# Top-k search of a sparse-attention layer: ties settled tile by tile, the long bit search in a branch of its own

## The chip, the cores and the metric

The kernel runs on one core of one Trainium2 chip. TensorE (PE) multiplies matrices into PSUM, VectorE (DVE) and ScalarE (ACT) work elementwise, GpSimd (POOL) does the same more slowly, SyncE (SP) issues the DMA transfers. Each engine executes its own instructions strictly in the order in which they were written out, and waits on semaphores for the others. The metric is the device time of one execution in microseconds, the median over several runs.

## The reference

One layer of a streaming encoder, for 1024 prompt frames and 64 sample frames (which see 128 cached frames too): a half-step SwiGLU feed-forward block, one combined input projection, a sparse-attention branch and a convolution branch that are gated and merged, an output projection, a second feed-forward block, and a last norm. What the change touches is the choice of keys in the attention branch:

```python
score = jnp.einsum('bqh,bqhs->bqs', wi.astype(jnp.float32), jax.nn.relu(s))
score = jnp.where(admissible[None], score, -jnp.inf)
_, sel = lax.top_k(score, top)          # top = 256 for the prompt, 48 for the sample
valid = sel < limit[None, :, None]
kg = jax.vmap(lambda kb, ib: kb[ib])(k, sel)
vg = jax.vmap(lambda vb, ib: vb[ib])(v, sel)
```

Each query keeps its `top` best keys by an indexer score, the sum over eight heads of a weight times a ReLU. Where several keys have the same score at the border, `top_k` keeps those that come first. A score is exactly zero where all eight ReLUs are zero, so zeros can be tied. The prompt's rows whose `top` covers all admissible keys (the first 256) need no choice.

## The kernel before, in words

All products are made in three passes of split operands (`mm3`, L134 to L138: high by high, high by low, low by high; the copies and differences that split them are L118/L119 and L152/L153). The layer runs in stages: first feed-forward block, input projection piece by piece, indexer scores, search, attention, merge and output projection, second feed-forward block.

The keys are not gathered. Attention works on all keys of a tile of 128 queries, and the search writes a bias row for each query: 0 for a kept key, a huge negative number for the others. The scores of seven tiles stand in `Y` (L653): six prompt tiles with 384, 512, 640, 768, 896 and 1024 keys and the sample's tile of 64 rows with 192 keys, 832 rows in all. The search, L875 to L998, has these steps:

- Fifteen rounds on the upper 16 bits of the scores (L906 to L916) find, for each row, the upper half `hib` of the border score. ScalarE does this for the widest tile, VectorE for the other six.
- The lower halves of the scores that share this upper half are masked out and the eight largest taken (L930, L932). `thr` is the rank wanted among them. For ranks 1 to 7 the lower half of the border score is picked (`lob`), and the next one (`nxt`); for a rank of 8 or more neither is.
- `threshold()` (L939 to L944) joins the halves into the border score `sth`. A row whose `lob` and `nxt` don't differ is either tied or of a rank of 8 or more. The smallest difference over all rows becomes the one flag `deepi` (L947 to L954), by a transpose in 32 x 32 blocks, a reduction, three small copies and a reduction.
- L955 to L960 write the bias of every tile by one comparison, and count the scores below the border.
- If the flag is set (L961, L962), a branch on VectorE alone finds the lower half of every row anew in sixteen rounds, each of which counts over all seven tiles (L979), and then settles the ties of all tiles in seven passes a tile (L986 to L998): a count, an equality, a running sum, a limit, and three passes that turn the running sum into a bias.

The small tiles of the search stand in one PSUM tile, `srch` (L877), out of the pool `lgi`. The pools of PSUM of this stage are closed at L1026, and attention's pools take the same banks; so do the convolution's SBUF buffers (`cvp_`, `ep`, closed at L1025) go to attention's (`ap_`).

While the search runs, TensorE computes gates, 16 of them in 3 chunks of 24 matmul triples each (`gates`, L1013 to L1021: a weight load with its split on ScalarE and GpSimd, products, an eviction by ScalarE at L1019, a store). `GPRE` of them are written ahead of attention (L1023), the rest are the first steps of a background list that attention draws on between its own steps (L1276). GpSimd and ScalarE run the last part of the convolution in the same stretch: ScalarE scales a shifted row (L679), GpSimd adds it (L680).

The order of instructions on each engine is fixed before the run by a planner that goes by priorities and a timeline of its own. What stands in a branch is planned as one unit: nothing from outside is put between its instructions. The search has a raised priority (L875).

## Time and profile before

| what | value |
|---|---|
| median of three runs | 2552.09 us (2544.73 to 2552.24) |
| the profiled execution's own time | 2549.7 us |
| its span | 2547.9 us |
| TensorE busy | 2316.0 us (91%) |
| VectorE busy | 1847.4 us (73%) |
| ScalarE busy | 1164.8 us (46%) |
| GpSimd busy | 1435.6 us (56%) |
| the sixteen rounds' comparisons (L979, 112 of them) | 96.9 us of VectorE |

The span is the time from the first to the last instruction in the trace; the profiled execution took 1.8 us more, and 2.4 us less than the median. The page cuts the span into 40 slices and gives each engine's busy share in tenths. A row of a view of groups names line, engine, operation, output and inputs with their shapes, then the count, the sum of the busy time and the mean of one in nanoseconds. A row of the view of waits says which engine at which line waited for which other engine's line, the total, the number of times and the longest. In a timeline, the first two numbers are the start and the length in microseconds, and a bracket at the end gives the idle time before the instruction and what ended it.

### The profile page before, as it was taken

What the parts mean: (1) busy time and instruction counts of PE and PEld (TensorE: products, weight loads), DVE (VectorE), ACT (ScalarE), POOL (GpSimd) and SP (SyncE); (2) the same over time, 40 slices, a digit from 0 to 9 for tenths busy, and PEclk for the clock granted to TensorE, in tenths of its full rate; (3) what the DMA queues carried; (4) which work ended last, traced back from release to release, by engine and by line L of the source; (5) the groups of instructions that cost most, each with busy time, mean ns of one, the idle gap of its engine ahead of it and who ended that gap; (6) DMA issues with size and microseconds to landing.
All of it is one profiled execution on the core that took longest, in us unless ns stands there. A gap on an engine that the chain in (4) does not pass through costs nothing.

```text
span 2547.9 us, 44592 instructions
## 1 busy us (share of the span) xinstructions
PE 2316.0 (91%) x16762; PEld 2283.4 (90%) x16762; DVE 1847.4 (73%) x4138; ACT 1164.8 (46%) x2237; POOL 1435.6 (56%) x873
## 2 busy tenths in 40 slices
PE   7999999999999999993048989989999999999998
PEld 6999999999999999993048888979999999999998
DVE  7766678766673776899996788557776668767676
ACT  6433345443355568862014555444444345344343
POOL 5455566555466868796045345546555565555554
PEclk9999999999999999997569999989999999999999
DMA  5222323223234432331002245564222222323223
GB/s 181 109 96 96 108 100 118 84 92 108 91 114 137 138 118 87 124 125 46 0 23 68 85 154 164 185 218 144 100 100 92 84 100 84 105 105 118 90 93 110
DMA packets 130408, 273.46 MB, mean 107 GB/s; under 512 B 17936, under 2 KB 77200, under 8 KB 130192
## 3 DMA queue, kind: packets, MB, share of 16 engines
q1 hardware_dynamic: 130192, 270.61, 31.3%
q8 instruction: 132, 2.16, 0.3%
q14 instruction: 84, 0.69, 0.1%
HBM read 231.87 MB, written 38.75 MB: 106 GB/s over the span
## 4 chain that ended last, share of the span: by engine, by line
PE 71%; DVE 16%; DMA 4%; POOL 4%; issue 3%; ACT 2%; SPq 0%; DVEq 0%; ACTq 0%; POOLq 0%
PE ps L136 22%; PE ps L138 22%; PE ps L137 22%; DVE bias L979 4%; POOL ac L680 3%; DMA raw<-wf 1%; PE pt L1093 1%; DMA ga<-d_g 1%; DVE bias L901 1%; DVE ps L312 1%; DVE ga L1230 1%; PE ps L166 1%; DVE x L153 1%; DVE s L314 1%; DVE t L211 1%
## 5 line engine op out<-in xcount | busy, mean ns | idle before, releaser
L119 POOL TENSOR_TENSOR wlo<-raw,whi 128x1024 fp32r<-128x1024 f32 (+1 forms) x187 | 437.3, 2343 | 377.8 <-ACT whi L118 373.9
L136 PE MATMUL ps<-x,whi 128*128 128x272 f32 (+2 forms) x1544 | 484.5, 314 | 137.5 <-DVE sth L944 119.8
L136 PE MATMUL ps<-x,wp 128*128 128x272 f32 x1760 | 506.5, 289 | 3.2 <-ACT wp L152 3.2
L138 PE MATMUL ps<-x,wp 128*128 128x272 f32 x1760 | 503.6, 290 | 2.0 <-DVE wp L153 1.0
L137 PE MATMUL ps<-x,wp 128*128 128x272 f32 x1760 | 505.1, 288 | 0.0
L138 PE MATMUL ps<-x,wlo 128*128 128x272 f32 (+2 forms) x1544 | 481.9, 313 | 0.0
L136 PEld LDWEIGHTS ps<-x,whi 128*128 128x128 f32 x1544 | 294.4, 191 | 140.8 <-DVE sth L944 120.5
L137 PE MATMUL ps<-x,whi 128*128 128x272 f32 (+2 forms) x1334 | 413.7, 310 | 0.9 <-POOL x L153 0.9
L136 PE MATMUL ps<-gh,whi 128*128 128x272 f32 x1408 | 400.1, 289 | 5.6 <-DVE spare L284 3.5
L137 PE MATMUL ps<-gl,whi 128*128 128x272 f32 x1408 | 405.2, 289 | 0.0
L138 PE MATMUL ps<-gh,wlo 128*128 128x272 f32 x1408 | 404.2, 289 | 0.0
L680 POOL TENSOR_TENSOR ac<-ac,pd 128x559 f32<-128x559 f32 x180 | 287.0, 1595 | 157.7 <-ACT pd L679 132.3
L153 POOL TENSOR_TENSOR wlo<-raw,whi 128x1024 fp32r<-128x1024 f32 x88 | 221.4, 2517 | 256.2 <-ACT whi L152 256.2
L136 PEld LDWEIGHTS ps<-x,wp 128*128 128x128 f32 x1760 | 331.2, 188 | 4.2 <-ACT wp L152 4.0
L138 PEld LDWEIGHTS ps<-x,wp 128*128 128x128 f32 x1760 | 328.8, 188 | 3.9 <-DVE wp L153 2.7
L137 PEld LDWEIGHTS ps<-x,wp 128*128 128x128 f32 x1760 | 331.5, 188 | 0.0
L153 POOL TENSOR_TENSOR wp<-s,wp 128x512 fp32r<-128x512 f32 x176 | 256.6, 1458 | 103.3 <-ACT wp L152 103.3
L428 DVE SCALAR_TENSOR_TENSOR h<-ps,h 128x272 f32<-128x272 f32 x384 | 164.4, 438 | 186.9 <-PE ps L138 186.2
L138 PEld LDWEIGHTS ps<-x,wlo 128*128 128x128 f32 x1544 | 294.0, 191 | 1.2
L118 ACT ACTIVATE whi<-raw 128x1024 fp32r<-128x1024 f32 (+1 forms) x187 | 190.5, 1020 | 221.3 <-PE ps L137 110.3
L136 PEld LDWEIGHTS ps<-gh,whi 128*128 128x128 f32 x1408 | 263.5, 189 | 6.9 <-DVE spare L284 3.9
L138 PEld LDWEIGHTS ps<-gh,wlo 128*128 128x128 f32 x1408 | 266.3, 189 | 0.0
(264 smaller groups left out, 5035.6 us busy)
## 6 DMA issues: line engine op xcount, KB each, us to landing
raw<-wf SPq DMA_DIRECT2D x337, 512.0 KB, 3.3
raw<-wf SPq DMA_DIRECT2D x32, 384.0 KB, 3.0
d_g<-sg SPq DMA_DIRECT2D x32, 181.0 KB, 1.9
d_h<-h SPq DMA_DIRECT2D x2, 2176.0 KB, 10.5
y<-t SPq DMA_DIRECT2D x32, 136.0 KB, 1.9
raw<-d_q SPq DMA_DIRECT2D x32, 128.0 KB, 3.5
raw<-d_qi SPq DMA_DIRECT2D x24, 128.0 KB, 3.1
d_g<-sg SPq DMA_DIRECT2D x16, 182.0 KB, 3.3
```

The source lines that it names most:

```text
L118: nc.scalar.activation(hi[:, :n], raw[:, :n], AF.Copy)
L119: self.weng.tensor_tensor(lo[:, :n], raw[:, :n], hi[:, :n], op=ALU.subtract)
L136: t.matmul(out, wh, xh, start=first, stop=False)
L137: t.matmul(out, wh, xl, start=False, stop=False)
L138: t.matmul(out, wl, xh, start=False, stop=last)
L153: (eng or nc.vector).tensor_tensor(lo, x, hi, op=ALU.subtract)
L166: self.nc.tensor.matmul(ps[:, b * P:(b + 1) * P], x[:, t0:t0 + P], self.ones, start=i == 0, stop=i == len(tiles) - 1)
L211: self.nc.vector.scalar_tensor_tensor(x, h[:, k, t0:t0 + w], self.par[:, q:q + 1], r, op0=ALU.mult, op1=ALU.mult)
L312: nc.vector.tensor_tensor(s[2], a0, b0, op=ALU.subtract)
L428: nc.vector.scalar_tensor_tensor(x, p, 0.5, x, op0=ALU.mult, op1=ALU.add)
L680: nc.gpsimd.tensor_tensor(ac, ac, pd, op=ALU.add)
L979: nc.vector.scalar_tensor_tensor(spare(n), Y[:rows, y0:y0 + L], sgn[:rows, c1], cand[:rows, c1].to_broadcast([rows, L]), op0=ALU.mult, op1 ...
```

## The change

The branch behind the flag is cut into nine branches. Inside the outer one the differences `nxt` are copied, and an eighth column is added that says for each row whether its rank is 8 or more while the eighth largest lower half isn't zero (a "far" row). `flags()`, the old reduction made general for up to 32 columns, turns these into eight integers in `tiei`: is any row of this tile tied, and is any row far. A second branch, entered if there is a far row, holds the sixteen rounds as they were, and then writes the bias by a comparison anew. After it, seven branches, one for each tile and each behind a register load of its own, settle the ties of a tile that is flagged: an equality with its sum, two operations on one column, a running sum into a new buffer `rk`, a comparison with the number of ties wanted, and one pass into the bias. The new buffer takes 4 KB a partition. Besides, `GPRE` goes from 10 to 11: one gate more is written ahead of attention, and one less is in the background list.

```diff
@@ -44,7 +44,7 @@
 PAHEAD = 60
 TORD = (7, 6, 8, 5, 4, 3, 2, 1, 0)
 NLG, NPT = 3, 2
-GPRE = 10
+GPRE = 11
 MS = lambda nc: set()
 FILL = {7: 1, 6: 1, 8: 2, 5: 1, 4: 1, 3: 2, 2: 2, 1: 2, 0: 2}
 THI = 6000
@@ -778,6 +778,8 @@
             for j in range(8):
                 nc.gpsimd.memset(rank[:, :, j:j + 1], float(j + 1) if j < 7 else 99.0)
             deepi = kp.tile([1, 1], I32, name="deepi")
+            tiei = kp.tile([1, NT + 1], I32, name="tiei")
+            rk = kp.tile([P, 1024], F32, name="rk")
 
             def cols(g):
                 return slice(COL[g[0]], COL[g[-1]] + 1)
@@ -878,9 +880,9 @@
             thr, low_ = sb_[:, 0:NT], sb_[:, 16:16 + NT]
             hib, lob = sb_[:, 32:32 + NT], sb_[:, 48:48 + NT]
             top8, prod = (sb_[:, a0:a0 + 8 * NT].rearrange("p (n t) -> p n t", t=8) for a0 in (64, 128))
-            deep = sb_[:, 256:328]
-            mi0 = sb_[:, 336:336 + NT].bitcast(I32)
-            nc.vector.memset(sb_[:, 32:328], 0.0)
+            deep = sb_[:, 256:352]
+            mi0 = sb_[:, 352:352 + NT].bitcast(I32)
+            nc.vector.memset(sb_[:, 32:352], 0.0)
             nc.vector.tensor_copy(thr, thr0)
 
 
@@ -945,13 +947,21 @@
             threshold()
 
             nc.vector.tensor_tensor(nxt, lob, nxt, op=ALU.subtract)
+
+            def flags(src, first, dst):
+
+                w = src.shape[1]
+                f = [deep[:, first + 32 * i:first + 32 * i + 32] for i in range(3)]
+                nc.vector.transpose(f[1], f[0])
+                nc.vector.tensor_reduce(f[2][:, 0:1], f[1], axis=AX.X, op=ALU.min)
+                for q in range(1, 4):
+                    nc.vector.tensor_copy(f[2][0:w, q:q + 1], f[2][32 * q:32 * q + w, 0:1])
+                nc.vector.tensor_reduce(f[0][0:w, 0:1], f[2][0:w, 0:4], axis=AX.X, op=ALU.min)
+                nc.vector.transpose(f[1][0:32, :], f[0][0:32, :])
+                nc.vector.tensor_scalar(dst, f[1][0:1, 0:w], 0.5, None, op0=ALU.is_lt)
+
             nc.vector.tensor_reduce(deep[:, 0:1], nxt, axis=AX.X, op=ALU.min)
-            nc.vector.transpose(deep[:, 32:64], deep[:, 0:32])
-            nc.vector.tensor_reduce(deep[:, 64:65], deep[:, 32:64], axis=AX.X, op=ALU.min)
-            for q in range(1, 4):
-                nc.vector.tensor_copy(deep[0:1, 64 + q:65 + q], deep[32 * q:32 * q + 1, 64:65])
-            nc.vector.tensor_reduce(deep[0:1, 68:69], deep[0:1, 64:68], axis=AX.X, op=ALU.min)
-            nc.vector.tensor_scalar(deepi, deep[0:1, 68:69], 0.5, None, op0=ALU.is_lt)
+            flags(deep[:, 0:1], 0, deepi)
             for n in (5, 4, 6, 3, 2, 1, 0):
                 rows, y0, L = rows_of(n)
                 c1 = slice(COL[n], COL[n] + 1)
@@ -962,40 +972,61 @@
             with tc.If(more > 0):
 
 
-                nc.vector.tensor_scalar(flag, hib, float(1 << 15), None, op0=ALU.is_lt)
-                nc.vector.tensor_scalar(sgn, flag, 2.0, -1.0, op0=ALU.mult, op1=ALU.add)
-                nc.vector.tensor_tensor(thr, ktop, lmk, op=ALU.subtract)
-                nc.vector.tensor_tensor(thr, thr, flag, op=ALU.mult)
-                nc.vector.tensor_tensor(thr, thr, lmk, op=ALU.add)
-                nc.vector.memset(lob, 0.0)
-                nc.vector.tensor_copy(low_, lob)
-                for b in range(15, -1, -1):
-                    nc.vector.tensor_scalar(lob, low_, float(1 << b), None, op0=ALU.add)
+                nc.vector.tensor_copy(deep[:, 0:NT], nxt)
+                nc.vector.tensor_scalar(flag, thr, 7.5, None, op0=ALU.is_ge)
+                nc.vector.tensor_tensor(flag, flag, top8[:, :, 7], op=ALU.mult)
+                nc.vector.tensor_reduce(deep[:, NT:NT + 1], flag, axis=AX.X, op=ALU.max)
+                nc.vector.tensor_scalar(deep[:, NT:NT + 1], deep[:, NT:NT + 1], -1.0, 1.0, op0=ALU.mult, op1=ALU.add)
+                flags(deep[:, 0:NT + 1], 0, tiei)
+                far = nc.vector.value_load(tiei[:, NT:NT + 1], min_val=0, max_val=1)
+                with tc.If(far > 0):
+
+                    nc.vector.memset(tiei, 1)
+                    nc.vector.tensor_scalar(flag, hib, float(1 << 15), None, op0=ALU.is_lt)
+                    nc.vector.tensor_scalar(sgn, flag, 2.0, -1.0, op0=ALU.mult, op1=ALU.add)
+                    nc.vector.tensor_tensor(thr, ktop, lmk, op=ALU.subtract)
+                    nc.vector.tensor_tensor(thr, thr, flag, op=ALU.mult)
+                    nc.vector.tensor_tensor(thr, thr, lmk, op=ALU.add)
+                    nc.vector.memset(lob, 0.0)
+                    nc.vector.tensor_copy(low_, lob)
+                    for b in range(15, -1, -1):
+                        nc.vector.tensor_scalar(lob, low_, float(1 << b), None, op0=ALU.add)
+                        threshold()
+                        nc.vector.tensor_tensor(cand, sth, sgn, op=ALU.mult)
+                        for n in VT + (XT,):
+                            rows, y0, L = rows_of(n)
+                            c1 = slice(COL[n], COL[n] + 1)
+                            nc.vector.scalar_tensor_tensor(spare(n), Y[:rows, y0:y0 + L], sgn[:rows, c1],
+                                                           cand[:rows, c1].to_broadcast([rows, L]),
+                                                           op0=ALU.mult, op1=ALU.is_ge, accum_out=cnt[:rows, c1])
+                        nc.vector.tensor_tensor(flag, cnt, thr, op=ALU.is_ge)
+                        nc.vector.scalar_tensor_tensor(low_, flag, float(1 << b), low_, op0=ALU.mult, op1=ALU.add)
+                    nc.vector.tensor_copy(lob, low_)
                     threshold()
-                    nc.vector.tensor_tensor(cand, sth, sgn, op=ALU.mult)
                     for n in VT + (XT,):
                         rows, y0, L = rows_of(n)
                         c1 = slice(COL[n], COL[n] + 1)
-                        nc.vector.scalar_tensor_tensor(spare(n), Y[:rows, y0:y0 + L], sgn[:rows, c1],
-                                                       cand[:rows, c1].to_broadcast([rows, L]),
-                                                       op0=ALU.mult, op1=ALU.is_ge, accum_out=cnt[:rows, c1])
-                    nc.vector.tensor_tensor(flag, cnt, thr, op=ALU.is_ge)
-                    nc.vector.scalar_tensor_tensor(low_, flag, float(1 << b), low_, op0=ALU.mult, op1=ALU.add)
-                nc.vector.tensor_copy(lob, low_)
-                threshold()
-                for n in VT + (XT,):
+                        nc.vector.scalar_tensor_tensor(spare(n), Y[:rows, y0:y0 + L], sth[:rows, c1],
+                                                       negc[:rows].to_broadcast([rows, L]),
+                                                       op0=ALU.is_lt, op1=ALU.mult, accum_out=cnt[:rows, c1])
+
+                for n in (5, 6, 4, 3, 2, 1, 0):
                     rows, y0, L = rows_of(n)
-                    c1 = slice(COL[n], COL[n] + 1)
-                    y, b = Y[:rows, y0:y0 + L], spare(n)
-                    nc.vector.tensor_scalar(b, y, sth[:rows, c1], 0.0, op0=ALU.is_le, op1=ALU.add,
-                                            accum_out=cnt[:rows, c1])
-                    nc.vector.tensor_scalar(need[:rows, c1], cnt[:rows, c1], float(STILES[n][4] - L), None, op0=ALU.add)
-                    nc.vector.tensor_scalar(y, y, sth[:rows, c1], None, op0=ALU.is_equal)
-                    nc.vector.tensor_tensor_scan(y, y, y, 0.0, op0=ALU.add, op1=ALU.bypass)
-                    nc.vector.tensor_scalar(y, y, need[:rows, c1], -NEG, op0=ALU.min, op1=ALU.mult)
-                    nc.vector.scalar_tensor_tensor(b[:, 0:1], b[:, 0:1], NEG, y[:, 0:1], op0=ALU.mult, op1=ALU.add)
-                    nc.vector.tensor_tensor(y[:, 0:L - 1], y[:, 1:L], y[:, 0:L - 1], op=ALU.subtract)
-                    nc.vector.scalar_tensor_tensor(b[:, 1:L], b[:, 1:L], NEG, y[:, 0:L - 1], op0=ALU.mult, op1=ALU.add)
+                    c = COL[n]
+                    c1 = slice(c, c + 1)
+                    tied = nc.vector.value_load(tiei[:, c1], min_val=0, max_val=1)
+                    with tc.If(tied > 0):
+                        y, b = Y[:rows, y0:y0 + L], spare(n)
+                        nc.vector.tensor_scalar(y, y, sth[:rows, c1], 0.0, op0=ALU.is_equal, op1=ALU.add,
+                                                accum_out=need[:rows, c1])
+                        nc.vector.scalar_tensor_tensor(need[:rows, c1], cnt[:rows, c1], 1.0 / NEG, need[:rows, c1],
+                                                       op0=ALU.mult, op1=ALU.add)
+                        nc.vector.tensor_scalar(need[:rows, c1], need[:rows, c1], float(STILES[n][4] - L), None,
+                                                op0=ALU.add)
+                        nc.vector.tensor_tensor_scan(rk[:rows, :L], y, y, 0.0, op0=ALU.add, op1=ALU.bypass)
+                        nc.vector.scalar_tensor_tensor(y, rk[:rows, :L], need[:rows, c1], y,
+                                                       op0=ALU.is_gt, op1=ALU.mult)
+                        nc.vector.scalar_tensor_tensor(b, y, NEG, b, op0=ALU.mult, op1=ALU.add)
             hi.__exit__(None, None, None)
 
             K = [load_k(ak, 32 + 32 * g, str(g)) for g in range(2)]
```

## The prediction

> **What bounds the kernel now.** I read the sliced page first. A slice is 63.7 us.
>
> ```profile
> span 2547.9 us, 44592 instructions
> PE   7999999999999999993048989989999999999998
> DVE  7766678766673776899996788557776668767676
> PEclk9999999999999999997569999989999999999999
> ```
>
> TensorE is nearly always busy, except in slices 18 to 20, where VectorE is full and the granted clock drops to the lower of its levels. The waits between 1150 and 1400 us say who waited there (engine, line, releaser: total, times, longest):
>
> ```profile
> ACT sg L1019 <- PE ps L138: 124.0, 3, 122.0
> ...
> POOL ac L680 <- ACT pd L679: 120.5, 1, 120.5
> PE ps L136 <- DVE sth L944: 119.8, 1, 119.8
> ...
> PE lg L1066 <- ACT sg L1019: 10.7, 1, 10.7
> ...
> PE ps L136 <- ACT sg L1019: 8.4, 1, 8.4
> ...
> PE lg L1066 <- DVE mb L1069: 7.7, 1, 7.7
> ```
>
> These waits are one chain. TensorE wants to write chunk 31 of the gates (the first chunk of the eleventh) into a PSUM bank that the search still holds as `srch`; the last reader of it is the `threshold()` behind the sixteen rounds. ScalarE, in order, sits at that chunk's eviction, and the convolution's scaled copies (L679) stand behind it, so GpSimd starves too. TensorE's four idle stretches add up to 119.8 + 10.7 + 8.4 + 7.7 = 146.6 us. The timeline of VectorE shows what it did meanwhile (start, length):
>
> ```profile
> 1173.75 0.14 DVE L954 TENSOR_SCALAR deepi<-srch 1x1 int32<-1x1 f32 x1
> 1174.95 0.17 DVE L965 TENSOR_SCALAR flag<-srch 128x7 f32<-128x7 f32 x1 [1.05 <-ACT pd L679]
> ...
> 1192.06 1.15 DVE L979 SCALAR_TENSOR_TENSOR bias<-Y,sgn,cand 128x896 bf16<-128x896 f32 x1
> ...
> 1199.37 1.15 DVE L979 SCALAR_TENSOR_TENSOR bias<-Y,sgn,cand 128x896 bf16<-128x896 f32 x1
> ...
> 1301.41 0.17 DVE L944 TENSOR_TENSOR sth<-srch,mi 128x7 int32<-128x7 int32 x1
> ...
> 1340.29 5.14 DVE L998 SCALAR_TENSOR_TENSOR bias<-bias,Y 128x895 bf16<-128x895 bf16 x7
> 1349.05 0.69 DVE L1069 CUSTOM_DVE_ANT_0 pr<-lg,bias 128x512 f32<-128x512 f32 x1 [3.61 <-POOL wlo L119]
> ```
>
> The branch is entered at 1174.95. The rounds come every 1199.37 - 1192.06 = 7.31 us and end at 1301.6; the tie passes over all seven tiles end at 1345.4; the first softmax reduction of attention starts at 1349.05. It did not wait for VectorE's own search but for GpSimd's side, the convolution whose buffers attention takes over:
>
> ```profile
> 1182.68 5.75 POOL L680 TENSOR_TENSOR ac<-ac,pd 128x559 f32<-128x559 f32 x3
> 1308.93 19.80 POOL L680 TENSOR_TENSOR ac<-ac,pd 128x559 f32<-128x559 f32 x6 [120.50 <-ACT pd L679]
> 1328.69 2.56 POOL L119 TENSOR_TENSOR wlo<-raw,whi 128x1024 fp32r<-128x1024 f32 x1
> 1331.21 15.45 POOL L680 TENSOR_TENSOR ac<-ac,pd 128x559 f32<-128x559 f32 x3
> ```
>
> Nine adds and one weight split are left when GpSimd starves at 1188.4; the last add ends at 1346.66, and 2.4 us later (its store lands, the buffer comes free) attention starts.
>
> **The change, part by part.**
>
> *The data decide which branches run.* By the reference's formulas on its own inputs, in single as in double precision, two of the 832 searched rows are tied: one in the 1024-column tile, one in the 640-column tile, both with a threshold of exactly zero. No row with another threshold has a rank above 6 among scores that share its upper sixteen bits. So the outer branch is entered, as in the trace, the far branch is not, and two of the seven tie branches are.
>
> *VectorE's new path*, with prices from these rows:
>
> ```profile
> L994 DVE TENSOR_TENSOR_SCAN Y<-Y 128x1024 f32<-128x1024 f32 x1 | 2.3, 2255 | 0.0
> ...
> L994 DVE TENSOR_TENSOR_SCAN Y<-Y 128x640 f32<-128x640 f32 x1 | 1.5, 1454 | 0.0
> L990 DVE TENSOR_SCALAR_CACHE_REDUCE bias<-Y,sth 128x1024 bf16<-128x1024 f32 x1 | 1.3, 1266 | 0.0
> ...
> L998 DVE SCALAR_TENSOR_TENSOR bias<-bias,Y 128x1023 bf16<-128x1023 bf16 x1 | 1.2, 1204 | 0.0
> ...
> L990 DVE TENSOR_SCALAR_CACHE_REDUCE bias<-Y,sth 128x640 bf16<-128x640 f32 x1 | 0.9, 874 | 0.0
> ...
> L998 DVE SCALAR_TENSOR_TENSOR bias<-bias,Y 128x639 bf16<-128x639 bf16 x1 | 0.8, 804 | 0.0
> ...
> L949 DVE STREAM_TRANSPOSE srch<-srch 128x32 f32<-128x32 f32 x1 | 0.2, 218 | 0.0
> ```
>
> 1. The first flag gains a transpose, 0.2 us: it stands at 1174.1. Loading it and branching took 1174.95 - 1173.89 = 1.06 us; the body starts at 1175.2.
> 2. Five small operations, some 0.2 us each, 1.0 us; then the flags once more: two transposes (0.44), two reductions, three copies and a compare of up to 0.2 us each, 1.6 us in all. At 1177.8 `tiei` stands.
> 3. Eight loads with a branch (one far, seven tiles), 8 x 1.06 = 8.5 us. No jump over a body is in the trace. Below 0.5 us each (half of the row, part of the load overlapped) it would be 4 us; above, a jump may cost a transfer of code, which a rival prices. I take the row, since the same load stands in it.
> 4. The 1024-column tile: compare with a sum 1.27, two narrow operations 0.3, scan 2.26, and two passes of up to 1.27: 6.4 us. The 640-column tile: 0.87 + 0.3 + 1.45 + 0.87 + 0.80 = 4.3 us. Five other tiles: nothing.
>
> The search thus ends at 1177.8 + 8.5 + 10.7 = 1197 instead of 1345.4. The rounds removed were worth 1301.6 - 1175 = 126.6 us of this, the passes over untied tiles and the shorter tie code the rest.
>
> *The bank* `srch` comes free once the far test is passed, at about 1179 (or at 1197, if the skipped branch is accounted for only at the end), so ScalarE no longer sits 122 us before an eviction.
>
> *What is late next* is the convolution. From 1188.4 GpSimd owes nine adds and a split. How its adds go:
>
> ```profile
> 1128.28 1.40 POOL ac L680
> 1129.74 1.42 POOL ac L680
> ...
> L680 POOL TENSOR_TENSOR ac<-ac,pd x51: 1362/1402/11476, 1099.4 to 1335.2; 128x559 f32<-128x559 f32 x51
> ```
>
> In the chain of waits, fed by ScalarE without a stop, they come every 1.46 us. The longest, of 11.5 us, fell under the scans and the last passes, which the two shared: 1312.3 to 1323.8 lies over the seven scans, 1335.2 to 1346.6 over the passes of L996 to L998. Nine adds at 1.46 us are 13.1, the split 2.56: 15.7 us, so 1204.1. On top, two scans (3.7 us) may hold an add up for their length, and the two tiles' passes a little: between 0 and 8 us, of which I take 4. The convolution ends at about 1208, later than VectorE by 11 us, and attention's first reduction starts 2.4 us behind it, at 1210.5. That is 1349.05 - 1210.5 = 138.5 us earlier.
>
> *The clock.* TensorE's windows (busy, matmuls, granted clock):
>
> ```profile
> 1301.00:1306.00 5.00, 4.37 (x16) 0.57 0.00 0
> 1306.00:1311.00 5.00, 5.00 (x33) 1.00 0.12 41
> ...
> 1327.00:1332.00 5.00, 4.25 (x14) 0.50 0.20 74
> ...
> 1349.00:1354.00 5.00, 4.20 (x14) 0.59 0.23 65
> ```
>
> After each of the three stalls the engine starts again at the lower level: 16 matmuls where the next five microseconds hold 33. At full clock (0.152 us each) the 16 and the two times 14 would take 2.4 + 2.1 + 2.1 of the 12.8 us that they were busy, so the stalls cost some 6 us more than their length. With shorter gaps I expect about half back, 3 us.
>
> *The eleventh gate.* The price of TensorE's work in this region:
>
> ```profile
> 1050.00:1100.00 50.00, 50.00 (x306) 49.91 (x305) 44.27 (x123) 44.17 (x87) 40.25 (x25) 1.00 0.55 171
> ...
> 1400.00:1450.00 50.00, 46.92 (x350) 45.34 (x349) 31.57 (x84) 26.39 (x55) 15.69 (x7) 1.00 0.30 95
> ```
>
> 306 matmuls in 50 us are 0.163 us each; a gate has 3 chunks x 8 x 3 = 72, 11.8 us. It leaves attention, where TensorE is 94% busy, for the stretch of the search. The old order ran chunks 31 to 36 between the first and the second logits, 23.6 us of work; from 1188 to 1210 there are 22 us for the same six. So the gate fills no time that stands idle, unless some of the 10.7 us hole ahead takes it, and its weights come only with the split that ended at 1182.7. Its ScalarE evictions (3 x 0.55 us) and stores move with it, ahead of attention on ScalarE and SP; the convolution's copies wait 1.65 us at most for them, inside the 0 to 8 above. Between nothing and 11.8 us I take 1, nearest to nothing.
>
> *The sum.* 138.5 + 3 + 1 = 142.5 us. The profiled execution took 2549.7 us, 1.8 beyond its span and 2.4 under the median of 2552.09: 2549.7 - 142.5 = **2407 us**. A ceiling checks it: the four stalls and the clock are worth 146.6 + 6 = 153 us, so 2397 is the least, unless the gate's place gives more.
>
> [...] Only one row shows code being fetched:
>
> ```profile
> q8 instruction: 132, 2.16, 0.3%
> ```
>
> These are 2.16 MB / 132 = 16.4 KB a packet, and the trace shows no jump that waits for one. [...]
>
> **The rivals.**
>
> *Every jump costs a fetch.* In this kernel 16.4 KB would have to come in before VectorE goes on. Its ends: nothing, and the 2.4 us in which the convolution's store was done and its buffer free again. If six jumps (far and five tiles) cost the long end, and twice it where the queue is shared, the search ends at 1197 + 15 to 29 = 1212 to 1226, behind the convolution; attention starts some 2 to 16 us later: **2409 to 2423 us**. For it: such jumps are new. Against: they end in the same few hundred instructions, and the convolution covers the first 11 us.
>
> *Attention's start stays tied to a later point.* The engines' orders are written ahead of time by a planner that sees the whole branch body as one unit. If the convolution's remaining copies stand behind an eviction that waits for the bank, and the bank comes free only with the end of the branch at 1197, GpSimd starts its nine adds there: 1197 + 15.7 + 4 + 2.4 = 1219 at 1.46 us an add, and 1231 if they keep the pace of 19.80 / 6 = 3.3 us half of the time. The gain falls to 118 to 130, **2418 to 2430 us**. For it: exactly this tie held 120 us before. Against: the eleventh gate uses the older banks, so three more evictions pass before the one that can block.
>
> *All of it comes back.* The new order puts the gate's chunks into the 10.7 us hole and TensorE hardly idles: 153 us, and a few more from the gate: **2392 to 2397 us**. Against: the weights at 1182.7.
>
> *The far branch is taken.* One row of rank 8 or more with a low half that isn't zero is enough. Then nothing is removed but passes behind the rounds, and work is added: up to 3.9 us of flags and tests in front, the count again, and seven tile branches.
>
> ```profile
> L958 DVE SCALAR_TENSOR_TENSOR bias<-Y,sth,negc 128x1024 bf16<-128x1024 f32 (+6 forms) x7 | 9.5, 1404 | 0.0
> ```
>
> Behind the rounds the old tail took 1345.4 - 1301.6 = 43.8 us. The new one is the count (5.6 where L990 stood undisturbed, 9.5 here), the compare 5.6, narrow operations 2.2, scans 9.6, two passes of 5.1 to 6, tests 7.4: 40.6 to 46.3. VectorE would end 1 to 6 us later than before, and attention with it: **2551 to 2556 us**, slower than before by up to 6 where the gate gains nothing. Against it: ranks that end at 6, and the rounding of one kernel's scores shifts a rank by one, seldom two.
>
> *The change doesn't shorten the search* otherwise only if `tiei` flagged every tile: between the two tiles priced above lie 5.5 ns a column and 0.8 us a tile, so the other five with 2752 columns cost 19 us and put VectorE at 1216, 2413 us, inside the first rival.
>
> **How the numbers follow.** The sum above holds in 0.50 (its own range 2398 to 2417), the fetch in 0.17, the later tie in 0.17, all back in 0.12, the far branch in 0.04. The range leaves the far branch and the outermost ends of the others: **2392 to 2430 us**. A change under 0.3% (7.7 us) can't be told from none here. All cases but the far branch lie 120 us or more below 2552; the far branch ends within 0.3% mostly (0.03), or beyond it (0.01). So faster 0.96, same 0.03, slower 0.01.
>
> **What would show each step.** In the profile after: no row of the rounds' compare; two scans, of 1024 and 640 columns; eight register loads of 1 us, at most, some 1178 to 1190; VectorE's last search pass near 1197; GpSimd's last convolution add near 1208 with no gap of over 10 us before it; the first softmax reduction at 1210 and the first transposes of probabilities 16 us behind; TensorE's waits in this stretch under 20 us and its clock at 0.9 or more in every slice; 33 gate evictions ahead of the first logits. Idle VectorE of 2 us or more at a test would show fetches. It would be wrong if the scan appears seven times, if TensorE still waits over 30 us for `srch`, or if attention itself runs longer than before from its first reduction to its last, for want of the gate's filler.

## The result, and the profile after

| | before | after |
|---|---|---|
| median (lowest to highest) | 2552.16 us (2544.73 to 2552.24) | 2402.84 us (2398.74 to 2404.17) |
| ratio of after to before | | 0.9419, 95% interval 0.9399 to 0.9439 |
| profiled execution, its span | 2549.7, 2547.9 us | 2398.74, 2397.0 us |
| first softmax reduction of attention | 1349.05 us | 1209.52 us |
| transposes of probabilities, first to last | 1364.8 to 1674.6 us | 1223.2 to 1524.9 us |

The kernel is 149.3 us faster by the medians; the forecast was 2407 us. The sliced page of after (a slice is 59.9 us):

```profile
span 2397.0 us, 44237 instructions
...
PE   7999999999999999999799999899999999999998
...
DVE  7766677666668287689846986568766678676676
PEclk9999999999999999999899999999999999999999
```

The three slices in which TensorE had 3, 0 and 4 tenths are gone; behind the first slice, the same in both, the lowest is one 7, and the granted clock falls below 9 tenths in one slice only. The waits of after between 1150 and 1300 us (engine, line, releaser: total, times, longest):

```profile
ACT pd L679 <- POOL ac L680: 31.3, 20, 4.3
...
PE lg L1097 <- ACT sg L1050: 12.7, 1, 12.7
...
DVE pr L1100 <- DMA d_dc<-ac: 8.2, 1, 8.2
...
PE lg L1097 <- DVE mb L1100: 1.7, 1, 1.7
```

TensorE's idle time there is 12.7 + 1.7 = 14.4 us where it was 146.6. No wait of over 5 us of the convolution's two engines on each other is left. VectorE waits 8.2 us for the convolution's last store, and 4.25 and 2.81 us for its own sequencer (`DVEq`) at the tests, as the brackets in its timeline say:

```profile
1177.21 0.15 DVE L961 TENSOR_SCALAR tiei<-srch 1x8 int32<-1x8 f32 x1
1181.62 1.28 DVE L1020 TENSOR_SCALAR_CACHE_REDUCE Y<-Y,sth 128x1024 f32<-128x1024 f32 x1 [4.25 <-DVEq L982]
...
1182.94 1.34 DVE L1022 SCALAR_TENSOR_TENSOR need<-cnt,need 128x1 f32<-128x1 f32 x1
1184.21 2.28 DVE L1026 TENSOR_TENSOR_SCAN rk<-Y 128x1024 f32<-128x1024 f32 x1
...
1186.57 2.15 DVE L1027 SCALAR_TENSOR_TENSOR Y<-rk,need,Y 128x1024 f32<-128x1024 f32 x1
1188.76 2.27 DVE L1029 SCALAR_TENSOR_TENSOR bias<-Y,bias 128x1024 bf16<-128x1024 f32 x1
1193.84 0.88 DVE L1020 TENSOR_SCALAR_CACHE_REDUCE Y<-Y,sth 128x640 f32<-128x640 f32 x1 [2.81 <-DVEq L1018]
...
1197.55 1.78 DVE L1027 SCALAR_TENSOR_TENSOR Y<-rk,need,Y 128x640 f32<-128x640 f32 x1
1199.37 1.91 DVE L1029 SCALAR_TENSOR_TENSOR bias<-Y,bias 128x640 bf16<-128x640 f32 x1
1209.52 0.69 DVE L1100 CUSTOM_DVE_ANT_0 pr<-lg,bias 128x512 f32<-128x512 f32 x1 [8.24 <-DMA d_dc<-ac]
```

The rounds are gone, two tiles are settled, and the search ends at 1201.3. GpSimd beside it:

```profile
1163.28 3.38 POOL L119 TENSOR_TENSOR wlo<-raw,whi 128x1024 fp32r<-128x1024 f32 x1
...
1181.45 12.27 POOL L680 TENSOR_TENSOR ac<-ac,pd 128x559 f32<-128x559 f32 x6
1193.68 2.38 POOL L119 TENSOR_TENSOR wlo<-raw,whi 128x1024 fp32r<-128x1024 f32 x1
1196.01 10.96 POOL L680 TENSOR_TENSOR ac<-ac,pd 128x559 f32<-128x559 f32 x6
```

The last add ends at 1206.97 and attention starts 2.55 us later (2.39 in before). That gives 1349.05 - 1209.52 = 139.5 us. The rest of the profiled executions' 2549.7 - 2398.74 = 151.0 us lies elsewhere. The windows of TensorE, first before, then after (stretch, length, busy and matmuls, granted clock, DMA share, GB/s):

```profile
1165.00:1170.00 5.00, 3.24 (x20) 1.00 0.42 142
1170.00:1175.00 5.00, 0.00 (x0) 0.72 0.00 0
1175.00:1180.00 5.00, 1.09 (x3) 0.50 0.16 57
```

```profile
1165.00:1170.00 5.00, 5.00 (x32) 1.00 0.40 142
1170.00:1175.00 5.00, 5.00 (x32) 1.00 0.01 3
1175.00:1180.00 5.00, 4.50 (x28) 1.00 0.22 76
1180.00:1185.00 5.00, 0.00 (x0) 0.65 0.45 143
```

From 1168 to 1179 TensorE stood still before, and is full after: that is the eleventh gate, 72 matmuls (a chunk of a gate is 24 matmuls, that is eight triples; the description of the kernel calls it 24 triples). A hole of some 12.7 us comes behind it (10.7 before). By the first sections of the two pages TensorE's 16762 matmuls were busy 2316.0 us before and 2301.6 after. So the spans' difference of 150.9 us is 14.4 us less of busy time, for the same matmuls, and 136.5 less of idle time.

### The profile page after: what moved, and what is told of

Read it like the earlier page. It is cut to its first block, busy times and chain, and to the rows that moved or that the text cites. A ratio compares the mean times of both kernels' runs of the same rounds, so it can differ in the third digit from the quotient of the medians.

```text
span 2397.0 us, 44237 instructions
## 1 busy us (share of the span) xinstructions
PE 2301.6 (96%) x16762; PEld 2271.2 (95%) x16762; DVE 1697.7 (71%) x3739; ACT 1165.6 (49%) x2237; POOL 1418.3 (59%) x873
## 4 chain that ended last, share of the span: by engine, by line
PE 74%; DVE 11%; DMA 5%; POOL 4%; issue 3%; ACT 2%; SPq 0%; DVEq 0%; ACTq 0%; POOLq 0%
PE ps L138 23%; PE ps L136 23%; PE ps L137 23%; POOL ac L680 4%; DMA raw<-wf 1%; DMA ga<-d_g 1%; PE lgi L833 1%; PE pt L1124 1%; PE lgi L834 1%; DVE ps L312 1%; PE ps L166 1%; DVE ga L1261 1%; DVE bias L903 1%; DVE pr L1100 1%; DVE s L314 1%
## 5 line engine op out<-in xcount | busy, mean ns | idle before, releaser
L680 POOL TENSOR_TENSOR ac<-ac,pd 128x559 f32<-128x559 f32 x180 | 269.9, 1499 | 36.4 <-ACT ac L675 12.3
## 6 DMA issues: line engine op xcount, KB each, us to landing
d_h<-h SPq DMA_DIRECT2D x2, 2176.0 KB, 10.8
```

The costliest lines, as they stand in the source:

```text
L680: nc.gpsimd.tensor_tensor(ac, ac, pd, op=ALU.add)
```

## The experiments

`again` is the changed kernel, run once more unchanged beside the first three; the runs from `a_far` on had only the kernel before beside them, whose median lay between 2550.4 and 2555.2 us from batch to batch. So a difference of 3 us to `again` or to after is not clear of noise there. Three questions: what the gate is worth, what sets attention's start and whether this still sets the end, and what the new branches cost.

| run | edit | median (range), us | first reduction | span of its profile |
|---|---|---|---|---|
| again | after, unchanged | 2403.07 (2401.83 to 2408.27) | 1210.4 | 2402.8 |
| a_g10 | after, `GPRE` 10 | 2415.06 (2413.21 to 2415.97) | 1214.2 | 2413.6 |
| b_g11 | before, `GPRE` 11 | 2545.15 (2540.59 to 2548.19) | 1348.7 | 2546.4 |
| a_g12 | after, `GPRE` 12 | 2410.24 (2408.26 to 2414.29) | 1210.7 | 2406.5 |
| a_far | far flag forced | 2546.61 (2540.19 to 2550.56) | 1350.1 | 2539.2 |
| a_ties | all tie flags forced | 2419.95 (2418.37 to 2423.41) | 1226.9 | 2421.6 |
| a_none | no tie flag | 2400.32 (2398.02 to 2402.57) | 1205.4 | 2399.3 |
| a_conv6 | six taps fewer | 2405.15 (2402.23 to 2411.04) | 1202.1 | 2402.2 |
| b_sbuf | before, `srch` in SBUF | 2549.44 (2545.21 to 2553.57) | 1350.1 | 2550.1 |
| a_banks | attention's PSUM pools in another order | 2406.08 (2403.65 to 2414.94) | 1212.0 | 2413.1 |
| a_short | after, short code in the far branch | 2402.31 (one run) | 1210.0 | 2400.5 |
| a_pd4 | four `pd` buffers | 2411.39 (2409.7 to 2414.91) | 1209.6 | 2413.1 |

### The gate: taken out of after, put into before

The changed kernel once more, unchanged:

> The changed kernel itself once more, as the measure for the others of this batch. Every theory: 2399 to 2405 us.

```diff
-GPRE = 11
+GPRE = 10
```

> The changed kernel with GPRE back at 10, so the new search alone. Theory A (the 8 us by which attention became shorter are the eleventh gate, which left a stretch where TensorE is busy for one where it idled): 7 to 11 us slower than the changed kernel, 2410 to 2413 us, attention's transposes span 308 to 311 us instead of 301.7. Theory B (the forecast: the gate fills no idle time and is worth 1 us; attention is shorter by its higher granted clock): 2403 to 2405 us, attention's transposes span 301 to 303.

The diff of the second run is the reverse of this, in the kernel before.

> The kernel before with GPRE at 11, so the gate alone. Theory A: the gate's 11.8 us come out of attention and go into the stall of 120 us, 2540 to 2545 us. Theory B: the start of attention is set by the search, and the gate changes nothing, 2550 to 2553 us.

Without its gate the changed kernel takes 2415.06 - 2403.07 = 12.0 us more. The gate alone makes the kernel before faster: 2545.15 against 2555.18 beside it, ratio 0.9955 (0.9940 to 0.9969), 10.0 us. So its move is worth 10 to 12 us in either order of the search, a little more than theory A gave in the changed kernel and at the end of its range in the kernel before. Each edit also makes the planner write another order of all that follows, so the price is one of the move with its order. The microseconds do not lie in the hole. Waits of TensorE ahead of attention in `a_g10`, and a window there:

```profile
PE lg L1097 <- ACT sg L1050: 12.0, 1, 12.0
PE lg L1097 <- DVE mb L1100: 1.9, 2, 1.4
```

```profile
1170.00:1175.00 5.00, 0.43 (x3) 1.00 0.30 107
```

Without the gate TensorE idles 13.9 us here, with it 14.4: the hole stays and only stands one gate later. In `b_g11` its waits are 114.3, 21.2 and 12.8 us, 148.3 in all for 146.6. The gain comes behind, in attention. `a_g10` starts attention 3.8 us later than `again`, but this is made up: by 1300 us TensorE had done 8925 matmuls in `a_g10`, 8926 in `again` and 8932 in after, each with all 16 gates, and 92, 90 and 92 transposes of probabilities. By 1400 it had done 9500, 9566 and 9580, with 198, 208 and 212 transposes (all counted in windows from the span's start). At `again`'s pace of 640 matmuls in these 100 us, 66 fewer are some 10 us, and they fall behind the last gate. Windows of TensorE, `a_g10`, then after:

```profile
1320.00:1360.00 40.00, 37.05 (x230) 0.96 0.45 134
1360.00:1400.00 40.00, 33.96 (x219) 0.87 0.47 139
```

```profile
1320.00:1360.00 40.00, 37.53 (x259) 1.00 0.57 171
1360.00:1400.00 40.00, 36.29 (x252) 1.00 0.51 153
```

The steps in a window need not be the same ones, but with about the same busy time `a_g10` gets through 449 matmuls, after through 511, at a higher granted clock and with 2.8 us less idle. (`again`, with the gate, has 505 and a clock of 1.00 and 0.96.) The transposes, from first to last, in the same two kernels (line, count, ns min/median/max, first and last start):

```profile
L1124 PE MATMUL pt<-ident,pr x304: 216/272/446, 1229.5 to 1543.7; 128*128 128x128 f32 x144, 64*128 64x64 f32 x4, 64*64 64x64 f32 x4
```

```profile
L1124 PE MATMUL pt<-ident,pr x304: 216/272/476, 1223.2 to 1524.9; 128*128 128x128 f32 x144, 64*128 64x64 f32 x4, 64*64 64x64 f32 x4
```

They span 314.2 us without the gate and 301.7 with it (303.4 in `again`, 309.8 in before). Over the whole span `a_g10`'s TensorE is busy 2313.0 us and idle 100.6, `again`'s 2306.1 and 96.7: of their 10.8 us 6.9 are busy time for the same matmuls, 3.9 idle. So the gate's price is one of how attention runs behind it. In `b_g11` this can't be seen: its profiled execution (2548.19 us) was the slowest of its six, and its transposes span 307.3 us.

A second gate more was tried too:

```diff
-GPRE = 11
+GPRE = 12
```

> The changed kernel with a twelfth gate ahead of attention. Theory A extended (TensorE still idles 12.7 us ahead of the first logits, which a gate more could fill): 2392 to 2398 us. Rival: the evictions of the gates are late on ScalarE, behind the convolution's copies, so one gate more only waits there as well, and its three evictions and one weight split delay the convolution by 3 to 5 us: 2403 to 2409 us.

It costs 7 us, a microsecond more than the rival's range. TensorE's longest wait ahead of attention is 15.4 us in it, not shorter than 12.7, so the twelfth gate fills no idle time there, and attention runs no better for it: its transposes span 303.5 us, as in `again`, but begin and end 4.5 us later.

### The tie flags: which side sets attention's start

```diff
                 far = nc.vector.value_load(tiei[:, NT:NT + 1], min_val=0, max_val=1)
# a_far, ahead of this line:
+                nc.vector.memset(tiei[:, NT:NT + 1], 1)
# a_ties:
+                nc.vector.memset(tiei[:, 0:NT], 1)
# a_none:
+                nc.vector.memset(tiei[:, 0:NT], 0)
```

> The changed kernel with the far flag set by hand, so the sixteen rounds run and the far branch writes the bias once more (the outcome is the same). Theory (the forecast's far rival, now with the gate's worth as the gate alone gave it, 2545 us): VectorE ends 1 to 6 us later than in the kernel before, 2546 to 2551 us. Rival (passes behind the rounds run beside GpSimd's adds and take up to twice as long, as the two tie branches showed): 2554 to 2560 us.

> The changed kernel with all seven tie flags set by hand, so five tiles more go through tie code that changes nothing in them. Theory (the convolution sets attention's start and VectorE had 7 us to spare): five tiles more cost 19 us at undisturbed prices and 35 us at the prices measured beside GpSimd, less 7: 2415 to 2431 us. Rival (VectorE is far from the path, TensorE's own work decides): 2403 to 2406 us.

> The changed kernel with all seven tie flags cleared by hand: the two tied rows keep more keys than they should, that is the only part left out. Theory (the convolution sets attention's start): VectorE ends 17 us earlier, the start comes earlier only by what the tie passes slowed the adds, 0 to 5 us, and the time is 2398 to 2403 us. Rival (the search still sets the start): the 17 us show, 2386 to 2390 us.

All three came out in their intervals. `a_far` measures the fourth rival, for this kernel's own data would never enter the far branch:

```profile
1350.07 0.69 DVE L1101 CUSTOM_DVE_ANT_0 pr<-lg,bias 128x512 f32<-128x512 f32 x1 [1.00 <-DVE bias L1030]
```

VectorE's search ends 1.00 us before this row, at 1349.07, which is 3.7 us later than the old 1345.4, and attention now follows VectorE's last pass, not the convolution. The time is 0.9983 of before (0.9973 to 0.9993): nothing lost, the gate included. `a_ties` prices five tiles more: VectorE ends at 1225.9, which is 24.6 later than in after, attention starts 17.3 later, and the time is 16.9 over `again`. A later start is paid in full. `a_none` starts attention 4.1 us earlier than after, and its median is 2.8 us under `again`, which is within the noise. What became shorter in it is TensorE's hole ahead of the logits. Waits of TensorE in `a_none`, 1160 to 1420:

```profile
PE lg L1098 <- ACT sg L1051: 9.7, 1, 9.7
```

In after this was 12.7. The eviction that ends it stands on ScalarE between the convolution's scaled copies, which wait for GpSimd's adds; in `a_none` six of the adds ahead of it take 8.58 us instead of 12.27, and it starts at 1188.80 instead of 1191.59. So some 3 us of the hole are, as read from these rows, the adds that the tie passes slow.

### Does the convolution's end still set the time?

```diff
-                    for j in range(1, CW):
+                    for j in range(1, CW - 6 if (t, s0) == (2, 559) else CW):
```

> The changed kernel without the last six taps of the convolution in the last half of its third channel group (part of the computation is left out), so that GpSimd is done some 11 us sooner. Theory 1 (the convolution sets attention's start, and the start the end): attention starts at VectorE's end, 6 to 7 us earlier, 2396 to 2398 us. Theory 2 (TensorE is full from 1195 us on, so an earlier start has nothing to give): attention may start earlier, the time stays at 2401 to 2404 us.

Timeline of VectorE in `a_conv6`:

```profile
1198.23 0.83 DVE L1029 SCALAR_TENSOR_TENSOR bias<-Y,bias 128x640 bf16<-128x640 f32 x1
1202.07 0.69 DVE L1100 CUSTOM_DVE_ANT_0 pr<-lg,bias 128x512 f32<-128x512 f32 x1 [3.01 <-ACT qt L691]
```

Attention starts 7.4 us earlier than in after, and nothing of it is in the time (2405.15 against 2403.07): theory 1 fell, theory 2 came within 1.2 us of its range. The transposes of probabilities begin 6.6 us earlier (1216.6) and end 2.5 us later (1527.4). TensorE says why: by 1250 us it had done 8612 matmuls in after, 8603 in `again` and 8594 in `a_conv6`. Its hole is 12.7 us here as in after, and from 1200 to 1250 it was busy for 50.00 us in after and 48.30 here, so there was next to no idle time that an earlier reduction could have filled. Attention's first reduction was placed by the convolution, as forecast, but at this point it sets the end no more: from here on a later start costs (`a_ties`), and one that is up to 7 us earlier gives nothing.

### The bank, before and after

The search's small tiles were moved out of the PSUM bank, in the kernel before:

```diff
-            sb_ = lgi.tile([P, 512], F32, name="srch", tag="lgi")
+            sb_ = kp.tile([P, 512], F32, name="srch")
```

> The kernel before with the search's small tiles in SBUF instead of a PSUM bank. Theory (TensorE's 120 us were a wait for that bank): the wait for it is gone, six chunks of gates run in the stall (23.6 us and the slow restart of 2 us), then TensorE waits for the first softmax reduction behind the search: 2523 to 2530 us. Rival (the bias is what all waits for, the bank only the place where it shows): 2548 to 2553 us.

Waits of TensorE in `b_sbuf`, 1160 to 1420:

```profile
PE lg L1066 <- DVE mb L1069: 142.5, 1, 142.5
PE lg L1066 <- ACT sg L1019: 7.7, 1, 7.7
```

My theory, a gain of 20 to 30 us, fell; the rival holds. Nothing waits for `srch` any more, the six gate chunks run early, and all of the idle time gathers at the next thing that needs the search, attention's first maximum. With a third wait of 0.6 the total is 150.8 us where it was 146.6; the ratio is 0.9994 (0.9983 to 1.0006). The bank was where the wait showed; what everything waited for was the bias.

The same for the hole that is left in the changed kernel, by opening attention's pools in another order (`psf` before `lg`, so that other banks go to the first logits):

```diff
-            lgp = self.pool(at_es, "lg", NLG, space=PS)
-            psf = self.pool(at_es, "psf", 7 - NLG - NPT, space=PS)
 ...
+            psf = self.pool(at_es, "psf", 7 - NLG - NPT, space=PS)
+            lgp = self.pool(at_es, "lg", NLG, space=PS)
```

> The changed kernel with attention's four PSUM pools opened in another order (psa, pv, psf, lg instead of lg, psf, psa, pv), so that the first logits take banks of the score stage, which are free, and not banks that wait for the gates' evictions on ScalarE. Theory (what is left is TensorE's own idle time, and the hole of 12.7 us ahead of the logits waits for an eviction): the hole falls to 0 to 6 us, 2391 to 2397 us. Rival (the convolution's end sets attention's start, and TensorE only waits later): the waits move to the first reductions, 2400 to 2404 us.

```profile
PE ps L136 <- ACT sg L1050: 9.5, 1, 9.5
```

The hole is 9.5 us instead of 12.7, at another place, and there is no gain: two runs lie at 2414 to 2415 us and three at 2403.7 to 2406.1. The theory fell, and the median lies above the rival's range too.

### The buffers of the convolution's copies

ScalarE's evictions stand behind its copies `pd`, and these wait for GpSimd (the 31.3 us above). Two buffers more should let ScalarE run ahead:

```diff
-                        pd = cvp_.tile([P, 559], F32, name="pd", tag="pd", bufs=2)
+                        pd = cvp_.tile([P, 559], F32, name="pd", tag="pd", bufs=4)
```

> The changed kernel with four buffers instead of two for the convolution's scaled copies, so that ScalarE can run two copies further ahead of GpSimd's adds and reaches the gates' evictions sooner. Theory (TensorE's own idle time is what is left, and the 12.7 us hole waits for an eviction that stands behind such copies): the hole falls by two adds of 1.5 to 2 us, to some 9 us, and the time to 2398 to 2400 us; the adds themselves end no later. Rival (as with the other order of the pools, the wait only moves): 2401 to 2406 us.

The hole is 14.6 us, not shorter, and the time 8.3 us longer than `again`, outside both forecasts. Since the planner wrote another order for the whole stretch, this doesn't clear the copies as a cause. Where the time went can be seen in the profiled run, the slowest of the five: by 1550 us TensorE had done 10378 matmuls in it and in `again` alike, by 1600 it had done 10602 and 10658. There, at the end of attention, the merge loads small pieces of the gates. Waits of TensorE at 1495 to 1575, then the chain of waits and SyncE's queue in the same stretch:

```profile
PE ps L136 <- DVE ga L1260: 17.6, 3, 13.2
```

```profile
1548.42 11.29 DMA ga<-d_g
```

```profile
1547.77 0.57 SPq L1350 DMA_DIRECT2D h<-d_h  x1
1548.42 3.50 SPq L1255 DMA_DIRECT2D ga<-d_g  x1
```

The gate's load of 181 KB (3.8 us in the median of after, 2.4 in the kernel before) was issued behind a large prefetch of L1350 (1448 to 1456 KB in after) and took 11.3 us. TensorE's longest wait for such a load (`ga`) was 1.6 us in after, 1.5 in `again`, 12.7 in the profiled run of `a_banks`, which is the slowest of its five, and 13.2 here. A few microseconds gained ahead of attention can be lost again at this place.

### The jump over the far branch

```diff
-                    for b in range(15, -1, -1):
+                    for b in range(0, -1, -1):
```

> The changed kernel with one round instead of sixteen in the far branch, which is not entered (left out are fifteen rounds that do not run). Theory (the 4.25 us from tiei to the first tie pass hold a fetch of code of 2.9 us, for the jump over some 350 instructions): with some 40 instructions to jump over they fall to 1.4 us. Rival (the load and the bookkeeping of a skipped branch cost it at any length): 4 us or more. The time in both: 2400 to 2405 us, since VectorE is not on the path.

The sequencer's rows of L982 (the far test) in after, then VectorE in `a_short`:

```profile
L982 DVEq COMPARE_BRANCH  x1: 67/67/67, 1177.8 to 1177.8; - x1
L982 DVEq EVENT_SEMAPHORE  x1: 21/21/21, 1180.7 to 1180.7; - x1
```

```profile
1177.64 0.15 DVE L961 TENSOR_SCALAR tiei<-srch 1x8 int32<-1x8 f32 x1
1179.36 1.28 DVE L1020 TENSOR_SCALAR_CACHE_REDUCE Y<-Y,sth 128x1024 f32<-128x1024 f32 x1 [1.57 <-DVEq L982]
```

With the far branch's code short, the gap in front of the first pass is 1.57 us instead of 4.25. So the long jump took 2.7 us more here; in after, 2.9 us pass between the branch and the sequencer's next row. The trace of after shows a load of code in this gap. The page of before has two rows of queues that fetch instructions. The prediction read the one of `q8`; this is the other:

```profile
q14 instruction: 84, 0.69, 0.1%
```

These are 8.2 KB a packet. In after one such packet starts at 1178.8, a microsecond behind the branch, and the next at 1181.3. That they hold the code behind the jump is read from these times. In the time of the kernel the shorter gap can't be seen (2402.31, a single run, against 2403.07 and 2402.84): the search ends ahead of the convolution with and without it.

## Why the prediction was right, and where not

**The data and the branches: right.** Two scans, of 1024 and 640 columns, and no round.

**Up to `tiei`: right**, 1177.36 where 1177.8 was forecast.

**Eight loads with a branch, 8.5 us: right in the sum, wrong in the parts.** Measured: 4.25 us to the first pass, 2.81 for the four tests between the two tiles, and about 1.0 for the last two, whose last load starts at 1201.7: 8.1 in all. A short test costs 2.81 / 4 = 0.7 us, less than the 1.06 taken, and the far one has 2.7 us on top, with a load of code in them. The trace of after has one stall with a load of code beside it, at the jump over the far body: 2.9 us between two rows of the sequencer, with a packet of code between them. From 1181.6 to 1200 us, over the four tests between the two tiles, no such packet starts. The first rival, a fetch at every jump, is out; the packet whose size it used, 16.4 KB, was that of `q8`.

**The two tiles' passes, 10.7 us: this term was mis-sized.** They took 1181.62 to 1191.03 and 1193.84 to 1201.28, 9.4 + 7.4 = 16.8. The scans kept their price (2.28 against 2.26). The four passes with two wide inputs and the two narrow operations at L1022 didn't: 2.15 + 2.27 + 1.78 + 1.91 us against 2 x 1.27 + 0.87 + 0.80, and 1.34 + 1.31 against some 0.2 each. The prices came from rows ahead of GpSimd's adds (L990) or in which the add was the one that took longer (L994, L998; 11.48 us for the longest); here each of these operations ended only behind the instruction that GpSimd was at when it started, by 0.01 to 1.08 us (the last section has the times). So the search ended at 1201.3, not 1197. As it still ended 5.7 us ahead of the convolution, the miss cost nothing beyond what it took from the adds.

**Nine adds, a split and 4 us of sharing: right.** Convolution's end 1206.97 for 1208, attention's start 1209.5 for 1210.5, 139.5 us for 138.5. The twelve adds in the rows above took 23.23 / 12 = 1.94 us each; over nine this is 4.3 us more than at 1.46. That the time would follow this start one for one was not shown by it: `a_conv6` started 7.4 us earlier for nothing. TensorE's own waits, which became 146.6 - 14.4 = 132.2 us shorter, bind as closely here; that the start's 138.5 us were so near the time is in part luck.

**The sum without the gate, 138.5 + 3: right in size.** `a_g10` is this kernel: 2555.18 - 2415.06 = 140.1 us by the medians of one batch where 141.5 was forecast. The profiled executions differ by less, 2549.7 - 2415.35 = 134.4 us, and its attention starts 1349.05 - 1214.24 = 134.8 us earlier, so the match to 1.4 us is closer than the record bears out. The clock's 3 us are in it as well: TensorE's busy time, for the same matmuls, is 2316.0 us in before and 2313.0 in `a_g10`. One sign of being wrong did come in this kernel: its attention runs longer than before, 314.2 us from first to last transpose where before has 309.8.

**The eleventh gate, 1 us: this step failed; it is worth 10 to 12.** The step says that "the gate fills no time that stands idle", so that its move is worth next to nothing, and that "its weights come only with the split that ended at 1182.7". The second half is wrong: that split belonged to a later gate, the eleventh's is the one before it (in after at 1163.28 to 1166.66), and its 72 matmuls run from 1168 on. The first half is right: TensorE's idle time ahead of attention is the same with it and without it. Wrong is what was concluded. The forecast priced the move by the place where the gate went, and left the place that it came from at nothing, though it names attention as 94% busy there. With one gate less among its steps attention gets from its first to its last transpose in 10.8 to 12.5 us less, at a higher clock (0.96 to 1.00 for 0.87, from 1360 to 1400 us), and no idle time ahead of it was filled for that. The other end that the prediction kept, 11.8 us, is close to the measured value, but by luck: it was the gate's own work, which is done by 1300 us in both kernels, while the difference arises behind that.

**The sum.** 142.5 were forecast; the profiled executions differ by 151.0, the medians of the first comparison by 149.3, those beside `again` by 152.1 = 140.1 + 12.0. What the sum lacks, 7 to 10 us, is in the gate's term.

**The rivals.** No eviction blocked the convolution, so the second isn't there. The third, 2392 to 2397 us, came near the time by another way than it said: TensorE still idles 14.4 us. The far branch would have been neither slower nor faster by more than 0.3%: `a_far` is 3.8 us below before, where the forecast had 2551 to 2556 with the gate taken as nothing.

**Open** is why attention runs at a lower clock and with more waits when one gate more stands among its steps; `a_g12` shows that it isn't a rule of one gate less, so much faster. Open, too, is what the hole of 12.7 us would be worth if it were gone. Some 3 us of it are adds slowed by the tie passes (`a_none`); neither other banks nor more buffers removed the rest, and both brought a new order with losses later on. No run was made that slows only the loads of L1255 or moves only the prefetches of L1350, so that these collide is read from the traces, not shown by an edit.

## What to carry to other kernels

A row that says "waits for a bank" names the place; ask what the next wait is if the bank were free, before a price is put on it. A piece of work that is moved has two prices, one at the place where it goes and one at the place that it leaves; price both, and undo the move by itself, since idle time alone didn't show this one. A stall shortened by 150 us shifts what binds: test with one edit that lengthens and one that shortens the new bound, since the two need not answer alike.

## What the runs showed of the hardware

**The tie passes on VectorE and GpSimd's additions lengthened each other.** In `a_conv6` GpSimd has no adds left, and the two wide passes over 640 columns took 0.89 and 0.83 us where they took 1.78 and 1.91 in after. In the other direction, without tie passes, six adds of `a_none` take 8.58 us where they took 12.27:

```profile
1181.47 8.58 POOL L680 TENSOR_TENSOR ac<-ac,pd 128x559 f32<-128x559 f32 x6
```

A pass over a single column took longer as well. VectorE in `a_ties`, then GpSimd:

```profile
1213.88 1.41 DVE L1023 SCALAR_TENSOR_TENSOR need<-cnt,need 128x1 f32<-128x1 f32 x1
...
1219.77 0.16 DVE L1023 SCALAR_TENSOR_TENSOR need<-cnt,need 128x1 f32<-128x1 f32 x1
```

```profile
1212.20 3.08 POOL L119 TENSOR_TENSOR wlo<-raw,whi 128x1024 fp32r<-128x1024 f32 x1
```

The narrow operation ends, to 0.01 us, as GpSimd's split ends (1215.29 and 1215.28), and the same operation takes 0.16 us later, when GpSimd is done. In `a_conv6` it stood beside a split too (1194.53, 1.30 us long) and ended with it, at 1195.83 for 1195.82. Both times it ended with one instruction of GpSimd. The wide passes ended behind one too. In after the adds that ran when they started end at 1187.64, 1189.95, 1198.65 and 1200.60 (the rows above join six adds to one); both passes over 1024 columns end 1.08 us behind that, at 1188.72 and 1191.03, both over 640 columns 0.68 us behind it. What the two engines share is not shown, only the times. As far as these rows go, the one that started second took longer. The scan over 1024 columns (1184.21) started as an add ended and kept its price; the add that started behind it, at 1184.35, took 3.29 us where the one ahead of it took 1.36.

**The jump over the far branch's some 350 instructions took 2.7 to 2.9 us (4.25 - 1.57, and the 2.9 of the sequencer's rows in after), a jump over a tile's few about 0.7 with its load (2.81 / 4).**

**Two issues took SyncE long in `a_pd4`.** Behind two of the large prefetches, whose own issues took 0.57 and 0.56 us, those of the next small loads took 3.50 (L1255) and 3.54 (L1257, 1552.63). In after the issues of L1255 take 0.32 us in the median and 0.72 at most.
